# The second layer's first FFN product as whole float32 matmuls instead of three matmuls of split parts

## The chip, the cores and the metric

The kernel runs on one core of one Trainium2 chip. A core has a tensor engine (PE, with PEld for its loads of stationary operands), a vector engine (DVE), a scalar engine (ACT), GpSimd (POOL) and a queue engine (SP) that issues most transfers here. The metric is the device time of one execution in microseconds (us); lower is better. Two executions of the kernel before took 2526.02 and 2526.43 us, median 2526.22 us.

## The reference

The reference is a trunk of two residual layers over 256 tokens of width 2048, all in float32. Each layer has a mixer (layer 0: retention and neighbourhood attention; layer 1: differential attention), a cross-attention into 256 memory tokens and a SwiGLU feed-forward network (FFN). What matters here is the FFN and its place:

```python
def swiglu_ffn(h, w_in, w_out):
    g, u = jnp.split(h @ w_in, 2, axis=-1)
    return (jax.nn.silu(g) * u) @ w_out

for i in range(DEPTH):                 # DEPTH = 2
    ...
    x = x + memory_cross_attention(rms_norm(x, norm_xattn_g[i]), m, ...)
    x = x + swiglu_ffn(rms_norm(x, norm_ffn_g[i]), w_ffn_in[i], w_ffn_out[i])
```

`h` is 256 x 2048, `w_ffn_in[i]` is 2048 x 11264 and `w_ffn_out[i]` is 5632 x 2048. The first FFN product is `h @ w_in`.

## The kernel before

**Split products.** The large products are not made of float32 matmuls. Each float32 operand is split into a high part, which is the value rounded to the type float32r, and a low part, which is the rest, also in float32r. One product of a 128x128 stationary tile and a 128x512 moving tile then takes three matmuls that add into the same accumulator: high by high, high by low, low by high (lines 318, 319, 320). In the FFN product the stationary operand is `hT`, the normed and transposed activations (`hTfh` and `hTfl` in the profile), and the moving operand is the weights (`wh` and `wl`). The whole-float32 form of a matmul occurs in one place only, the retention heads (line 539, `pa_r <- vh, dm`), where both operands are plain float32 tiles of 128x128.

**The weight stream.** All weights go through one stream. `plan` lists the products as phases; a phase is a matrix, its row groups of 512, its column groups of 512 and the order of its units. A unit is two row tiles of 128 against one group of 512 columns, for both halves of the 256 tokens. `prepare()` brings the next unit: for each second unit it allocates one of three `raw` buffers of 1 MB (pool `rawp`) and issues the transfer on SP (line 284); then ACT makes the high part `wh` by a cast (line 291) and DVE makes the low part `wl` by a subtraction (line 293). Both have pools of three buffers. `gemm()` keeps three units prepared (`LOOK = 2`, and the one in use), and makes a unit's matmuls: 2 halves of the tokens x 2 row tiles x 3 parts = 12.

**The order around it.** `Side` holds side work (transposes of the activations, attention heads, norms) and places steps of it between units. A scheduler then sets the order within each engine. The first FFN product of a layer runs in three groups of column blocks, `FFN_GROUPS = ((0, 4), (4, 8), (8, 11))`, each followed by the part of the second FFN product that uses them. It has 22 column groups x 8 units = 176 units per layer, so 176 x 4 = 704 pairs of tiles, each with three matmuls. A column group ends in `epi_in` (silu on ACT, line 782, or a multiplication on DVE), which reads the accumulator.

**The activations.** `feed()` transposes blocks of `x`, and `gained()` writes them with the norm's gain into `hT`: the high part by ACT (line 347), the low part by DVE (line 348). For the FFN of one layer there are 16 such pairs.

Of the kernel before, what the change touches and what calls it, by code (L numbers as in the profile page):

```python
# [10 lines left out]
F32 = mybir.dt.float32  # L11
# [5 lines left out]
P = 128  # L17
D = 2048
T = 256
# [8 lines left out]


class Side:  # L30
    """Steps of generators, placed after units of the weight stream. A step yields the units to wait before
    the next one, or (units, what has to hold)."""

    CAP = 5

# [43 lines left out]
def trunk_kernel(  # L79
# [8 lines left out]
    nc = tc.nc  # L88
# [18 lines left out]
    ps_t = pool("ps_t", 2, space=bass.MemoryType.PSUM)  # L107
    ps_a = pool("ps_a", 2, space=bass.MemoryType.PSUM)

    # ---------------------------------------------------------------- loads  # L110
    x_sb = const.tile([P, 2, D], F32, name="x_sb")
    x_v = x[0].rearrange("(t p) d -> p t d", p=P)
    def load_x(b):
# [12 lines left out]
    nc.gpsimd.iota(tdiff, pattern=[[-P, 2], [1, T]], base=0, channel_multiplier=-1,  # L126
                   allow_small_or_imprecise_dtypes=True)
    tabs = tdiff
    # columns of the grid outside the window of each query's column, in both halves of the partitions
    wmask = const.tile([P, 64], F32, name="wmask")  # L130
    nc.gpsimd.memset(wmask, 0.0)
    for q in range(2):
# [42 lines left out]
            nc.vector.tensor_scalar(hcol[:, c:c + n], hcol[:, c:c + n], f, None, op0=ALU.mult)  # L175

    def decays():
        # log_sigmoid(y) = -(max(-y, 0) + log1p(exp(-|y|))), log1p(e) = 2 atanh(e / (2 + e))
        dec = sm.tile([P, 16], F32, name="dec")
        nc.scalar.dma_start(dec[:, 0:8], dec_f.broadcast_to([P, 8]))  # L180
        nc.scalar.dma_start(dec[:, 8:16], dec_b.broadcast_to([P, 8]))
        e_t = sm.tile([P, 16], F32, name="e_t")
        z_t = sm.tile([P, 16], F32, name="z_t")
        z2 = sm.tile([P, 16], F32, name="z2")
        pl = sm.tile([P, 16], F32, name="pl")
        nc.vector.scalar_tensor_tensor(out=e_t, in0=dec, scalar=-1.0, in1=dec, op0=ALU.mult, op1=ALU.min)
        nc.scalar.activation(e_t, e_t, AF.Exp)
        nc.vector.tensor_scalar(z_t, e_t, 2.0, None, op0=ALU.add)
        nc.vector.reciprocal(z_t, z_t)
        nc.vector.tensor_mul(z_t, z_t, e_t)  # L190
        nc.vector.tensor_mul(z2, z_t, z_t)
        nc.vector.tensor_scalar(pl, z2, 2.0 / 17.0, 2.0 / 15.0, op0=ALU.mult, op1=ALU.add)
        for n in (13, 11, 9, 7, 5, 3, 1):
            nc.vector.tensor_mul(pl, pl, z2)
            nc.vector.tensor_scalar(pl, pl, 2.0 / n, None, op0=ALU.add)
        nc.vector.tensor_mul(pl, pl, z_t)
        nc.vector.tensor_scalar(nlg, dec, -1.0, 0.0, op0=ALU.mult, op1=ALU.max)
        nc.vector.tensor_add(nlg, nlg, pl)
        nc.vector.tensor_scalar(lg, nlg, -1.0, None, op0=ALU.mult)
        return  # L200
        yield
# [14 lines left out]
        return  # L216
        yield

    # ------------------------------------------------------------- helpers
    def pair(which, name):  # L220
        hi = big.tile([P, 16, T], F32R, tag=f"{which}h", name=f"{name}h")
        lo = big.tile([P, 16, T], F32R, tag=f"{which}l", name=f"{name}l")
# [6 lines left out]
    LOOK = 2  # L229

    def woven(nblocks, nu, early, lead=2):
        """The first `lead` blocks do their early units first."""
        head = [(b, u) for b in range(lead) for u in range(early)]
        head += [(b, u) for b in range(lead) for u in range(early, nu)]
        return head + [(b, u) for b in range(lead, nblocks) for u in range(nu)]

    # the weight stream: (matrix, row groups, column groups, order of (column group, unit))
    plan = []

    def phase(w2, rows, cols, order=None):  # L240
        nu = 2 * len(rows)
        plan.append((w2, rows, cols, order or [(b, u) for b in range(len(cols)) for u in range(nu)]))

    four = tuple(b * NB for b in range(4))
# [5 lines left out]
    for layer in range(2):  # L250
        j = layer // 2
        if layer % 2 == 0:
            phase(w_in_ab[j], K4, cols_ab, start)
            phase(w_out_ab[j], (1024, 1536, 0, 512), four, woven(4, 8, 6))
        else:
            phase(w_in_c[j], K4, cols_c, woven(len(cols_c), 8, 6))
            phase(w_out_c[j], K4, four, woven(4, 8, 6))
        phase(w_xkv[layer], K4, (0,))
        phase(w_xq[layer], K4, (0,))
        phase(w_xkv[layer], K4, (NB,))  # L260
        phase(w_xo[layer], (0,), four, woven(4, 2, 1))
        for g0, g1 in FFN_GROUPS:
            n = 2 * (g1 - g0)
            cols = [c + b * NB for b in range(g0, g1) for c in (0, HID)]
            phase(w_ffn_in[layer], K4, cols, woven(n, 8, 6) if g0 == 0 else None)
            phase(w_ffn_out[layer], tuple(b * NB for b in range(g0, g1)), four, woven(4, n, n - 2))
    units = [(i, b, u) for i, ph in enumerate(plan) for b, u in ph[3]]
    ahead = deque()
# [1 line left out]
    at = {"unit": 0, "phase": 0}  # L270

    def prepare():
        """The next unit of weights, two row groups of 128, in its two parts."""
        i, b, u = units[at["unit"]]
        w2, rows, cols, _ = plan[i]
        c, h = u // 2, u % 2
        if (i, b, c) not in raws:
            raw = raws[i, b, c] = rawp.tile([P, 4, NB], F32, name="raw")
            src = w2[rows[c]:rows[c] + 512, cols[b]:cols[b] + NB].rearrange("(k p) n -> p k n", p=P)
            if at["unit"] == 0:  # L280
                nc.sync.dma_start(raw[:, 0:2], src[:, 0:2])
                nc.sync.dma_start(raw[:, 2:4], src[:, 2:4])
            else:
                nc.sync.dma_start(raw, src)
        if at["unit"] in (1, 5, 9):
            load_x(at["unit"] // 4 + 1)
        raw = raws[i, b, c]
        if h:
            del raws[i, b, c]
        wh = hip.tile([P, 2, NB], F32R, name="wh")  # L290
        nc.scalar.copy(wh, raw[:, 2 * h:2 * h + 2])  # L291
        wl = lop.tile([P, 2, NB], F32R, name="wl")
        nc.vector.tensor_sub(wl, raw[:, 2 * h:2 * h + 2], wh)  # L293
        ahead.append((wh, wl))
        at["unit"] += 1

    def gemm(kts, src, epi, gate=None, steps=1):
# [5 lines left out]
        for b, u in order:  # L303
            side.drain((gate or {}).get(u, ()))
            if b not in accs:
                accs[b] = [ps_acc.tile([P, NB], F32, tag=f"acc{t}", name=f"acc{t}") for t in range(2)]
                left[b] = nu
            while len(ahead) <= LOOK and at["unit"] < len(units):
                prepare()
            wh, wl = ahead.popleft()  # L310
            acc = accs[b]
            first, left[b] = left[b] == nu, left[b] - 1
            last = left[b] == 0
            for t in range(2):
                ts = slice(t * P, (t + 1) * P)
                for j in range(2):
                    kt = kts[u // 2] + 2 * (u % 2) + j
                    nc.tensor.matmul(acc[t], lhsT=hi[:, kt, ts], rhs=wh[:, j], start=first and j == 0, stop=False)  # L318
                    nc.tensor.matmul(acc[t], lhsT=hi[:, kt, ts], rhs=wl[:, j], start=False, stop=False)  # L319
                    nc.tensor.matmul(acc[t], lhsT=lo[:, kt, ts], rhs=wh[:, j], start=False, stop=last and j == 1)  # L320
            if last:
                epi(b, acc)
            side.pump(steps)
# [19 lines left out]
        return pt  # L343

    def gained(dst, kt, src, g):
        hi, lo = dst[0][:, kt], dst[1][:, kt]
        nc.scalar.activation(hi, src, AF.Copy, scale=g)
        nc.vector.scalar_tensor_tensor(out=lo, in0=src, scalar=g, in1=hi.bitcast(F32),  # L348
# [15 lines left out]
        yield  # L364

    def feed_x(dst, b, gi, layer, ssr, wait=0):
        """The steps that bring block b of x, transposed and with its gain, into dst."""
        then = (lambda: finish_rstd(ssr)) if b == 3 else None
        t0 = side.add(feed(dst, b, 0, x_block(b), gi, layer, ssr), wait)
        return [t0, side.add(feed(dst, b, 1, x_block(b), gi, layer, ssr, then), wait + 1, finished([t0]))]  # L370
# [3 lines left out]
        nc.vector.tensor_sub(lo, src, hi)  # L374

    def product(out, lhs, rhs, start, stop):
        """out += lhs.T @ rhs, each given in its two parts."""
        (lh, ll), (rh, rl) = lhs, rhs
        nc.tensor.matmul(out, lhsT=lh, rhs=rh, start=start, stop=False)  # L379
        nc.tensor.matmul(out, lhsT=lh, rhs=rl, start=False, stop=False)  # L380
# [3 lines left out]
        return tuple(x[(slice(None),) + index] for x in pair)  # L384

    def gained_pair(dst, src, g):
        """Both parts of src * g."""
        hi, lo = dst
        nc.scalar.activation(hi, src, AF.Copy, scale=g)
        dims = "p a b -> p (a b)"  # L390
# [99 lines left out]
        return att_pair(pt)  # L490

    def attend(g, h, dst, kt, bias=None):
        """One head of softmax attention; g holds qT, kT and, later, v."""
        ps = scores(g["q"], g["k"], h)
        pr = att.tile([P, 2, T], F32, tag="att", name="pr")
        if bias is not None:
# [12 lines left out]
            product(po, part(v, s, slice(h * HD, (h + 1) * HD)), part(pT, s), s == 0, s == 1)  # L509
        split(dst[0][:, kt], dst[1][:, kt], po)  # L510

    # -------------------------------------------------------- even mixer
    def na_bias(j, gi, g, behind=None):
        bias = g["bias"] = m8.tile([P, 4, 2, T], F32, tag="m8", name="bias")
        if behind is not None:  # the table comes in behind what is needed sooner
            nc.gpsimd.tensor_copy(bias[:, 0, :, 0:8], behind.rearrange("p (t c) -> p t c", t=2))
        for t in range(2):
            for q in range(2):
# [83 lines left out]
        side.drain(tails[:1])  # L602
        return {6: tails}

    # --------------------------------------------------------- odd mixer
    def diff_head(g, hh, h, j, oT):
        slope = 2.0 ** (-8.0 * (h + 1) / 8)
        prs = []
# [57 lines left out]
            side.drain(groups[b]["tasks"])  # L666
        return {6: groups[3]["tasks"]}

    # ------------------------------------------------------------ norms
    def new_ss(name):  # L670
        return (sm.tile([P, 2, 4], F32, name=name), sm.tile([P, 2], F32, name=name + "r"),
                sm.tile([P, 2], F32, name=name + "q"))
# [11 lines left out]
        for t, xb in enumerate(x_block(b)):  # L684
            nc.vector.tensor_tensor(xb, acc[t], xb, op=ALU.add)

    # ------------------------------------------------------------ trunk
    which = "AB"
    hT = pair(which[0], "hT")
    ssr = new_ss("ssx")  # L690
# [8 lines left out]
    for layer in range(2):  # L699
# [50 lines left out]
        xo = (xo[:, 0], xo[:, 1])  # L750
        heads = [side.add(attend(g, h, xo, h), cond=prepared(g)) for h in range(4)]
        gemm(KT4, mT, epi_v, steps=2)
        hT = pair(B, "hTf")
        ssr = new_ss("ssx")
        tasks = []

# [82 lines left out]
```

## Time and profile before

| | |
|---|---|
| median of the runs, us | 2526.22 (2526.02 to 2526.43) |
| span of the profiled execution, us | 2523.3 |
| PE busy in the span, us (share) | 2506.5 (99%) |
| PEld busy, us (share) | 2077.9 (82%) |
| DVE busy, us (share) | 1428.8 (57%) |
| ACT busy, us (share) | 1191.3 (47%) |
| mean granted clock of the tensor engine | 1.000 |
| mean rate of the transfers | 185 GB/s |

The profiled execution's time is its span, 2523.3 us, from the first to the last instruction. The median of the runs is 2.9 us longer: what lies around the span. The duration of a matmul in the profile runs from its start to its modelled end. Matmuls overlap, so in a stream the distance from one start to the next (the pitch) is what one costs, and not its duration.

### The profile page before, as it was taken

Reading aid. Unit: us, or ns where it says so; the run is one execution under the profiler, and the core shown is the slowest. Engines: PE = TensorE matmul, PEld = TensorE weight load, DVE = VectorE, ACT = ScalarE, POOL = GpSimd, SP = SyncE. Lnnn points to the kernel's source line nnn. Section 1 sums busy time; section 2 is a strip of 40 time slices with the busy share of each in tenths; the row PEclk is TensorE's granted clock in tenths of the full one; section 3 lists DMA queues with packets and bytes.
Section 4 is the critical chain, followed back from the end, with each engine's and each line's share of the span. In section 5 each row is a group of like instructions: output and inputs, shape, how many; then the busy total and the mean of one; then the engine's idle time right before and its main releaser. Section 6 shows DMA issues by size and latency. Waiting matters only on the chain.

```text
span 2523.3 us, 28920 instructions
## 1 busy us (share of the span) xinstructions
PE 2506.5 (99%) x11603; PEld 2077.9 (82%) x11603; DVE 1428.8 (57%) x1686; ACT 1191.3 (47%) x1553; POOL 50.2 (2%) x56
## 2 busy tenths in 40 slices
PE   8999999999999999999999999999999999999999
PEld 6888888888888888888888888888888888888887
DVE  5775555674555445545557766757654545545454
ACT  5554455564443444344445545655544344443443
POOL 1000000000000000000000000000000000000000
PEclk9999999999999999999999999999999999999999
DMA  7555555545555555555555555554555565555555
GB/s 235 171 174 177 179 191 185 178 155 193 186 186 198 186 197 184 195 189 189 193 183 167 168 167 171 196 184 155 179 185 198 185 199 185 188 195 189 194 185 165
DMA packets 234509, 465.69 MB, mean 185 GB/s; under 512 B 7931, under 2 KB 8582, under 8 KB 234374
## 3 DMA queue, kind: packets, MB, share of 16 engines
q1 hardware_dynamic: 231552, 459.32, 55.3%
q0 software_dynamic: 640, 2.10, 0.4%
q10 hardware_dynamic: 2182, 2.42, 0.3%
q8 instruction: 91, 1.49, 0.3%
q14 instruction: 44, 0.36, 0.0%
HBM read 461.71 MB, written 2.10 MB: 184 GB/s over the span
## 4 chain that ended last, share of the span: by engine, by line
PE 97%; DMA 1%; DVE 1%; ACT 0%; POOL 0%; issue 0%; SPq 0%; ACTq 0%; DVEq 0%; POOLq 0%
PE acc L318 31%; PE acc L320 31%; PE acc L319 31%; PE pt L342 3%; PE pt L489 0%; PE pa_s L381 0%; PE pa_s L380 0%; PE pa_s L379 0%; DMA x_sb<-in_x 0%; DMA bias<-in_na_rpb 0%; PE pa_r L539 0%; DMA mb<-in_mem 0%; DMA lrow<-in_lambda_k 0%; DVE wl L293 0%; PE pa_o L381 0%
## 5 line engine op out<-in xcount | busy, mean ns | idle before, releaser
L293 DVE TENSOR_TENSOR wl<-raw,wh 128x1024 fp32r<-128x1024 f32 x864 | 1056.2, 1224 | 962.8 <-ACT wh L291 962.6
L291 ACT CAST wh<-raw 128x1024 fp32r<-128x1024 f32 x864 | 909.3, 1052 | 1178.0 <-PE acc L320 1158.8
L318 PE MATMUL acc<-wh,hTfh 128*128 128x512 f32 x1408 | 551.5, 392 | 0.0
L320 PE MATMUL acc<-wh,hTfl 128*128 128x512 f32 x1408 | 548.2, 389 | 0.0
L319 PE MATMUL acc<-wl,hTfh 128*128 128x512 f32 x1408 | 547.8, 389 | 0.0
L318 PE MATMUL acc<-wh,hTh 128*128 128x512 f32 x832 | 332.6, 400 | 2.7 <-DVE z L419 1.5
L320 PE MATMUL acc<-wh,hTl 128*128 128x512 f32 x832 | 325.7, 391 | 1.1 <-DVE hTl L348 1.0
L319 PE MATMUL acc<-wl,hTh 128*128 128x512 f32 x832 | 325.0, 391 | 0.0
L320 PEld LDWEIGHTS acc<-wh,hTfl 128*128 128x128 f32 x1408 | 264.3, 188 | 55.4
L319 PEld LDWEIGHTS acc<-wl,hTfh 128*128 128x128 f32 x1408 | 264.5, 188 | 53.7
L318 PEld LDWEIGHTS acc<-wh,hTfh 128*128 128x128 f32 x1408 | 264.4, 188 | 53.6
L318 PE MATMUL acc<-wh,aTh 128*128 128x512 f32 x704 | 275.5, 391 | 0.0
L320 PE MATMUL acc<-wh,aTl 128*128 128x512 f32 x704 | 274.4, 390 | 0.0
L319 PE MATMUL acc<-wl,aTh 128*128 128x512 f32 x704 | 274.1, 389 | 0.0
L320 PEld LDWEIGHTS acc<-wh,hTl 128*128 128x128 f32 x832 | 156.5, 188 | 36.3 <-DVE hTl L348 2.4
L318 PEld LDWEIGHTS acc<-wh,hTh 128*128 128x128 f32 x832 | 156.9, 189 | 33.2 <-issue 2.3
L319 PEld LDWEIGHTS acc<-wl,hTh 128*128 128x128 f32 x832 | 157.2, 189 | 28.6
L320 PEld LDWEIGHTS acc<-wh,aTl 128*128 128x128 f32 x704 | 132.3, 188 | 27.4
L319 PEld LDWEIGHTS acc<-wl,aTh 128*128 128x128 f32 x704 | 132.2, 188 | 26.9
L318 PEld LDWEIGHTS acc<-wh,aTh 128*128 128x128 f32 x704 | 132.2, 188 | 26.9
L318 PE MATMUL acc<-wh,oTh 128*128 128x512 f32 x256 | 101.9, 398 | 0.0
L320 PE MATMUL acc<-wh,oTl 128*128 128x512 f32 x256 | 99.9, 390 | 0.0
(193 smaller groups left out, 1915.7 us busy)
## 6 DMA issues: line engine op xcount, KB each, us to landing
raw<-in_w_ffn_in SPq DMA_DIRECT2D x176, 1024.0 KB, 5.1
raw<-in_w_ffn_out SPq DMA_DIRECT2D x88, 1024.0 KB, 5.1
raw<-in_w_in_ab SPq DMA_DIRECT2D x55, 1024.0 KB, 5.3
raw<-in_w_in_c SPq DMA_DIRECT2D x48, 1024.0 KB, 5.1
raw<-in_w_out_ab SPq DMA_DIRECT2D x16, 1024.0 KB, 5.1
raw<-in_w_xkv SPq DMA_DIRECT2D x16, 1024.0 KB, 5.0
raw<-in_w_out_c SPq DMA_DIRECT2D x16, 1024.0 KB, 5.2
raw<-in_w_xq SPq DMA_DIRECT2D x8, 1024.0 KB, 5.3
```

The source lines that it names most:

```text
L291: nc.scalar.copy(wh, raw[:, 2 * h:2 * h + 2])
L293: nc.vector.tensor_sub(wl, raw[:, 2 * h:2 * h + 2], wh)
L318: nc.tensor.matmul(acc[t], lhsT=hi[:, kt, ts], rhs=wh[:, j], start=first and j == 0, stop=False)
L319: nc.tensor.matmul(acc[t], lhsT=hi[:, kt, ts], rhs=wl[:, j], start=False, stop=False)
L320: nc.tensor.matmul(acc[t], lhsT=lo[:, kt, ts], rhs=wh[:, j], start=False, stop=last and j == 1)
L342: nc.tensor.transpose(pt[:, j, t * P:(t + 1) * P], srcs[t][:, c:c + P], ident)
```

## The change

The phases of the second layer's first FFN product are marked as whole. For these, `prepare()` makes no `wh` and `wl`; it hands the half of the `raw` buffer on as it is. `gemm()` then makes one matmul in float32, with the `raw` buffer as moving operand, for each three of before. The activations `hT` of this product are one float32 tile (`hTw`) without a low part, so `gained()` makes one instruction instead of two. The first layer and all other products keep the split.

```diff
-    def phase(w2, rows, cols, order=None):
+    whole = set()
+
+    def phase(w2, rows, cols, order=None, is_whole=False):
         nu = 2 * len(rows)
+        if is_whole:
+            whole.add(len(plan))
         plan.append((w2, rows, cols, order or [...]))
...
-            phase(w_ffn_in[layer], K4, cols, woven(n, 8, 6) if g0 == 0 else None)
+            phase(w_ffn_in[layer], K4, cols, woven(n, 8, 6) if g0 == 0 else None, is_whole=layer == 1)
...
         if h:
             del raws[i, b, c]
+        if i in whole:
+            ahead.append((raw[:, 2 * h:2 * h + 2], None))
+            at["unit"] += 1
+            return
         wh = hip.tile([P, 2, NB], F32R, name="wh")
...
                     kt = kts[u // 2] + 2 * (u % 2) + j
+                    if wl is None:
+                        nc.tensor.matmul(acc[t], lhsT=hi[:, kt, ts], rhs=wh[:, j], start=first and j == 0,
+                                         stop=last and j == 1)
+                        continue
                     nc.tensor.matmul(acc[t], lhsT=hi[:, kt, ts], rhs=wh[:, j], start=first and j == 0, stop=False)
...
     def gained(dst, kt, src, g):
+        if dst[1] is None:
+            nc.scalar.activation(dst[0][:, kt], src, AF.Copy, scale=g)
+            return
...
-        hT = pair(B, "hTf")
+        if layer == 0:
+            hT = pair(B, "hTf")
+        else:
+            hT = big.tile([P, 16, T], F32, tag=f"{B}h", name="hTw"), None
```

The rest of the edit takes out comments, which shifts line numbers: the weight transfer is line 288 after, the whole matmul line 327, the split ones 330 to 332, a transpose of `feed()` 354.

The first place is the start of the second layer's first FFN product on PE. `pt` are transposes of `x` for the last blocks of `hT`, `acc_...` the accumulators of the first column group for one half of the tokens each. Before, the rows read:

```order
L342 MATMUL pt<-ident,x_sb 128x128 x3
L318 MATMUL acc_13732<-wh,hTfh 128x512 [waits Activation_49]
L319 MATMUL acc_13732<-wl,hTfh 128x512
L320 MATMUL acc_13732<-wh,hTfl 128x512
L318 MATMUL acc_13732<-wh,hTfh 128x512
```

After the change the rows at the same place, with a whole unit between two lots of transposes, read:

```order
L354 MATMUL pt<-ident,x_sb 128x128 x3
L327 MATMUL acc_13711<-raw,hTw 128x512 [waits DMAHW3_49]
L327 MATMUL acc_13711<-raw,hTw 128x512
L327 MATMUL acc_13712<-raw,hTw 128x512 x2
L354 MATMUL pt<-ident,x_sb 128x128 [waits DVE_49,Activation_49]
L354 MATMUL pt<-ident,x_sb 128x128 [waits DVE_49]
L354 MATMUL pt<-ident,x_sb 128x128 x2
```

A unit is now four matmuls in the program where it was twelve, and the first of them waits for the transfer itself (`DMAHW3`) where the first of before waited for ACT's cast.

The second place is SP's queue where the first of the three groups ends and the second product's weights (`in_w_ffn_out`) begin. The names in brackets are what a transfer waits for: an earlier transfer's semaphore, and the engine that frees the buffer. Before:

```order
L284 DMA raw<-in_w_ffn_in 128x4x512 [waits DMAHW6_49,DVE_49]
L284 DMA raw<-in_w_ffn_in 128x4x512 [waits DMAHW7_49,DVE_49]
L284 DMA raw<-in_w_ffn_out 128x4x512 [waits DMAHW0_49,DVE_49]
L284 DMA raw<-in_w_ffn_out 128x4x512 [waits DMAHW1_49,DVE_49]
L284 DMA raw<-in_w_ffn_out 128x4x512 [waits DMAHW2_49,DVE_49]
L284 DMA raw<-in_w_ffn_out 128x4x512 [waits DMAHW3_49,DVE_49]
```

After:

```order
L288 DMA raw<-in_w_ffn_in 128x4x512 [waits DMAHW6_49,PE_49]
L288 DMA raw<-in_w_ffn_in 128x4x512 [waits DMAHW7_49,PE_49]
L288 DMA raw<-in_w_ffn_out 128x4x512 [waits DMAHW0_49,PE_49]
L288 DMA raw<-in_w_ffn_out 128x4x512 [waits DMAHW1_49,PE_49]
L288 DMA raw<-in_w_ffn_out 128x4x512 [waits DMAHW3_49,DVE_49]
L288 DMA raw<-in_w_ffn_out 128x4x512 [waits DMAHW2_49,PE_49]
L288 DMA raw<-in_w_ffn_out 128x4x512 [waits DMAHW4_49,DVE_49]
```

Inside the product, and for the first transfers behind it, a buffer is now freed by PE, when the last matmul that reads it is done, where DVE freed it when `wl` was made. The third and fourth transfers of the second product have changed places in the queue.

## The prediction

> **What bounds the kernel now.** I read the page first: its head, the clock row and the chain of work that ended last.
>
> ```profile
> span 2523.3 us, 28920 instructions
> PE 2506.5 (99%) x11603; PEld 2077.9 (82%) x11603; DVE 1428.8 (57%) x1686; ACT 1191.3 (47%) x1553; POOL 50.2 (2%) x56
> PEclk9999999999999999999999999999999999999999
> PE 97%; DMA 1%; DVE 1%; ACT 0%; POOL 0%; issue 0%; SPq 0%; ACTq 0%; DVEq 0%; POOLq 0%
> ```
>
> PE is busy 99% of the span, at its full granted clock, and 97% of the chain is PE. Work taken from another engine gives nothing here; PE's own time decides. The stretch that holds the changed product (from the end of the second layer's attention to the end) shows the same in the windows view. Its columns are the window, its length, then the busy time of each engine, clock, share and rate of the transfers.
>
> ```profile
> 1763.20:2523.30 760.10, 756.21 (x3397) 625.74 (x3397) 386.42 (x371) 322.17 (x351) 0.69 (x1) 1.00 0.57 187
> 2519.44 0.69 DVE x_sb L685
> ```
>
> Of 760.1 us PE is idle 3.9, and the chain's last row (start, duration) says that 2523.3 - 2519.4 = 3.9 us of the stretch lie behind PE's last work. So no stall is left there that the change could remove. The groups of the costliest instructions name the work:
>
> ```profile
> L293 DVE TENSOR_TENSOR wl<-raw,wh 128x1024 fp32r<-128x1024 f32 x864 | 1056.2, 1224 | 962.8 <-ACT wh L291 962.6
> L291 ACT CAST wh<-raw 128x1024 fp32r<-128x1024 f32 x864 | 909.3, 1052 | 1178.0 <-PE acc L320 1158.8
> L318 PE MATMUL acc<-wh,hTfh 128*128 128x512 f32 x1408 | 551.5, 392 | 0.0
> L320 PE MATMUL acc<-wh,hTfl 128*128 128x512 f32 x1408 | 548.2, 389 | 0.0
> L319 PE MATMUL acc<-wl,hTfh 128*128 128x512 f32 x1408 | 547.8, 389 | 0.0
> ```
>
> 1408 is both layers; the second has 704 triples. What a triple costs is its pitch, from the timeline (start, duration) inside the product:
>
> ```profile
> 1900.03 0.39 PE L318 MATMUL acc<-wh,hTfh 128*128 128x512 f32 x1
> 1900.25 0.39 PE L319 MATMUL acc<-wl,hTfh 128*128 128x512 f32 x1
> 1900.48 0.39 PE L320 MATMUL acc<-wh,hTfl 128*128 128x512 f32 x1
> 1900.71 0.39 PE L318 MATMUL acc<-wh,hTfh 128*128 128x512 f32 x1
> ...
> 1911.59 0.39 PE L318 MATMUL acc<-wh,hTfh 128*128 128x512 f32 x1
> ```
>
> 17 triples lie between the first row and the last: 11.56 / 17 = 0.680 us per triple, 0.2267 us per split matmul.
>
> **The change, part by part.** (1) It removes 704 triples, 704 x 0.680 = 478.7 us, all of it on the path.
>
> (2) It adds 704 whole float32 matmuls of 128x512. No row shows one of that size; the same form at 128 columns is line 539, and beside it stand the one-pass matmuls of 256 columns and the float32 transposes:
>
> ```profile
> L539 PE MATMUL pa_r<-vh,dm 128*128 128x128 f32 x64 | 8.9, 277 | 0.0
> L379 PE MATMUL pa_s<-kTh,qTh 128*128 128x256 f32 x64 | 18.0, 281 | 0.0
> L342 PE MATMUL pt<-ident,sg 128*128 128x128 f32 x192 | 28.7, 272 | 0.0
> L169 PE MATMUL pt_g<-ident,gr 96*128 96x96 f32 x1 | 0.2, 246 | 0.0
> 1353.47 0.28 PE L379 MATMUL pa_s<-kTh,qTh 128*128 128x256 f32 x1
> 1353.59 0.28 PE L380 MATMUL pa_s<-kTl,qTh 128*128 128x256 f32 x1
> 1353.71 0.28 PE L381 MATMUL pa_s<-kTh,qTl 128*128 128x256 f32 x1
> ```
>
> First, the number of instructions. Line 539 is called for 8 heads x 2 x 2 = 32 products and the trace has 64: a whole float32 matmul is two instructions on the chip, each with its load. Second, what one of them takes. The split matmuls have a pitch of 0.120 us at 256 columns and 0.2267 at 512, so a column of one pass costs 0.1067 / 256 = 0.417 ns and 13 ns are fixed. At 128 columns a one-pass matmul would then last 281 - 128 x 0.417 = 228 ns, but line 539 shows 277, the duration of 256 columns. The transposes agree: from 96 to 128 columns the duration grows by 26 ns, 0.81 ns per column, twice 0.417. I read this as two passes over the columns in each float32 instruction, four per product. Third, the fixed part, from the back-to-back row of line 539 (PE, and the loads that go with it):
>
> ```profile
> 242.56 0.94 PE L539 MATMUL pa_r<-vh,dm 128*128 128x128 f32 x6
> 242.55 0.74 PEld L539 LDWEIGHTS pa_r<-vh,dm 128*128 128x128 f32 x6 [0.29 <-ACT vh L461]
> L539 PEld LDWEIGHTS pa_r<-vh,dm 128*128 128x128 f32 x64 | 8.5, 191 | 1.2 <-ACT vh L461 0.6
> ```
>
> Six loads span 0.74 us and one lasts 0.191, so the pitch is 0.55 / 5 = 0.110 us for 128 columns. Two passes of 128 columns are 256 x 0.417 = 107 ns, which leaves 3 ns, not 13. For 512 columns the bounds are 1024 x 0.417 = 427 ns with nothing fixed, and 4 x 110 = 440 with the fixed part in each quarter. I take 427 + 3 = 430 ns, since the fixed part of line 539 is per instruction. A product then costs 0.860 us against 0.680, and the change 704 x 0.180 = +126.7 us (0.854: +122.5; 0.880: +140.8).
>
> The Trainium skill, in "FP8 and Floating Point Precision", section "TensorE Precision Notes", says that a true float32 matmul makes four passes, high and low of each side, the product of the two low parts included; three split matmuls leave that one out. By this rule the change cannot win, and line 539's doubled instructions with doubled durations agree. In "TensorE: Matmul & The Clock Gate", section "Back-to-back issue gap", it gives N / 2.4 + 2.5 ns for a warm matmul, 215.8 for 512 columns, where the trace has 226.7 for the split form, so the measurement decides there; as an estimate from that page, an instruction of two passes is 429.2 ns and the change 704 x (0.8584 - 0.680) = +125.6 us.
>
> (3) Loads: two per product instead of three. They were hidden (PEld overlaps PE), and at a pitch of 0.110 us one fits under 0.430 us of matmul. Zero; a load out in the open is a rival below.
>
> (4) ACT loses 176 casts of 1.052 us, DVE 176 subtractions of 1.224 us and 16 of the 32 low parts of activations:
>
> ```profile
> L348 DVE SCALAR_TENSOR_TENSOR hTfl<-pt,gcol,hTfh x32: 472/476/484, 547.2 to 1801.3; 128x256 fp32r<-128x256 f32 x32
> ```
>
> That is 185 us of ACT and 215 + 8 us of DVE. All of it lay beside PE (ACT 47%, DVE 57% busy). Zero.
>
> (5) The buffers. A `raw` buffer is now free only when PE has finished with it. Two units share a buffer and there are three, so a transfer for units 2r and 2r+1 starts at the end of unit 2r-5 and has four units of cover. A unit is four products, 3.44 us: 13.8 us of cover. The need:
>
> ```profile
> raw<-in_w_ffn_in SPq DMA_DIRECT2D x176, 1024.0 KB, 5.1
> L284 SPq DMA_DIRECT2D raw<-in_w_ffn_in x176: 367/368/368, 538.9 to 2431.1; - x176
> DMA to landing us min/median/max: 4.9/5.1/9.2
> ```
>
> 0.4 us to issue and 5.1 to land, 9.2 at worst: hidden. SP has nothing but weights in this stretch, so what queues behind a waiting transfer is the next weights, and PE waits for them last. The tightest place is where the second product starts: its third transfer (behind the fourth in the queue) needs the buffer of the last whole units, starts when they end, and its units are the fifth and sixth of that product. The cover is four split units of 4 x 0.680 = 2.72 us, 10.9 us; the need is 5.5, then 1.05 for the cast and 1.22 for the subtraction, 7.8 us. Zero, and if that cover is short, about the 2.3 us of preparation at each of three such places, 7 us at most.
>
> The sum: 2523.3 + 126.7 = 2650.0 us of span, and with the 2.9 us that the runs' median has above the span 2652.9. With the bounds and the 7 us of part 5, 2648.7 to 2674.0; I begin at 2646 for the hundredths by which the pitches are read.
>
> **The rivals.**
>
> *Faster: one pass per instruction.* If each of the two instructions streams its 512 columns once at today's pitch, a product costs 2 x 0.2267 = 0.453 us: 704 x (0.453 - 0.680) = -160 us, 2366 us. For it: the pitch of 0.110 us in line 539 could be that of the loads alone, and ends of matmuls are modelled. Against: the duration of 277 ns, and the transposes' slope. It decides where a product takes under 0.680 us, that is, an instruction under 0.340. 6%.
>
> *No change: three passes.* If the product of the two low parts is left out by the hardware, a product is 3 x 0.2135 + 0.006 = 0.647 us: 704 x (-0.033) = -23 us, 2503 us. Against: both instructions of line 539 last alike. 2%.
>
> *Slower: 13 ns in each pass.* If each of the four passes costs the 0.2267 us of today's matmul, a product is 0.907 us: +160 us, 2686 us. Against: the 0.110 us of line 539 leaves no room for that. 8%.
>
> *Slower: a load out in the open.* If the second load of a product waits for the first instruction's end, each of 1408 instructions pays 0.110 us: +155 us on top, 2808 us. Nothing of the kind shows in line 539, whose PE row has no idle time. 3%.
>
> *Slower: the weights come late.* If a buffer came free so late that one unit of cover was left, each of 88 transfers would cost 5.5 - 3.44 = 2.1 us: +181 us on top, 2834 us. It decides where landing takes over 13.4 us, above all landings seen. 2%.
>
> *The change does not do what it says:* the 704 matmuls run as one split matmul each, 704 x (0.2267 - 0.680) = -319 us, 2207 us. Line 539, from plain float32 tiles, is doubled, so hardly. 1%.
>
> **How the numbers follow.** The forecast has 78%, and its time is 2653 us. To leave out no more than 2 in 10 the range takes in the nearest rival, 2686: 2646 to 2688 holds 86%. About 2% (50 us) is what a measurement of this kernel tells from no change. Faster: 6 + 1 = 7%. Within 2%: 3%, with a point for what lies between the cases. Slower: the rest, 90%.
>
> **What the profile after would show.** 1408 instructions of line 327 in place of 2112, and 11603 - 704 = 10899 on PE; their pitch 0.430 us; PE still 99% busy at full clock, some 127 us longer; ACT near 1191 - 185 = 1006 us and DVE near 1429 - 215 - 8 = 1206 us, with no gain from it. A pitch near 0.227 or 0.453 gives the rival of that size; idle time of PE ahead of line 327 put down to `raw` gives the late weights; a granted clock under 1.00 in the stretch would be a cause that I have not priced. I am wrong if 512 columns of float32 take a different number of passes than the 128 of line 539.

## The result and the profile after

The changed kernel takes 2652.35 us (2651.98 to 2652.71) against 2526.22 us before: a ratio of 1.0498, 95% interval 1.0479 to 1.0518. It is slower by 126.1 us, where +126.7 us was forecast.

The head of the page after, its clock row, the chain by engine and by line, and the costliest groups of the changed product read:

```profile
span 2650.2 us, 26921 instructions
PE 2631.7 (99%) x10899; PEld 1949.3 (74%) x10899; DVE 1210.9 (46%) x1494; ACT 1008.6 (38%) x1377; POOL 50.2 (2%) x56
PEclk9999999999999999999999999999999999999999
PE 98%; DMA 1%; DVE 1%; ACT 0%; POOL 0%; issue 0%; ACTq 0%; SPq 0%; DVEq 0%; POOLq 0%
...
L327 PE MATMUL acc<-raw,hTw 128*128 128x512 f32 x1408 | 607.7, 592 | 0.0
L327 PEld LDWEIGHTS acc<-raw,hTw 128*128 128x128 f32 x1408 | 266.0, 190 | 326.9 <-issue 326.7
```

PE has 704 instructions less and 125.2 us more busy time (2631.7 against 2506.5). It still fills 99% of the span at its full clock, while DVE and ACT lost 217.9 and 182.7 us. The last column of the matmul row is PE's idle time ahead of it: 0.0 us in 1408 instructions. That rules out long waits, for `raw` say, but not short ones: a matmul lasts 592 ns to its modelled end and the next one starts after 429, so a wait of up to 163 ns would not show as idle time. It is the pitch that rules out the short ones. The loads' own idle time, 326.7 us put down to "issue", is the loads waiting their turn behind matmuls that have become longer.

The pitch is read from the chain in order of time (start, length, work):

```profile
1799.39 51.50 PE acc L327 x120
1850.89 0.44 PE pt L354 x4
1851.33 3.43 PE acc L327 x8
```

51.50 / 120 = 0.4292 us per instruction, 0.8584 us per product of two instructions, against 0.680 us for the triple: 704 x 0.1784 = +125.6 us. Two passes over 512 columns at the prediction's 0.417 ns are 427 ns, so some 2 ns of the 429 are left for all else: no load lies in the open. The span grew by 126.9 us, but about 2 us of that arose ahead of the changed product. In the view by tile, the last transfer of the weights just ahead of it is issued at 1763.6 us before (first row) and at 1765.5 us after:

```profile
L284 SPq DMA_DIRECT2D raw<-in_w_xo x8: 367/368/368, 512.0 to 1763.6; - x8
L288 SPq DMA_DIRECT2D raw<-in_w_xo x8: 367/368/368, 514.1 to 1765.5; - x8
```

The shift is there from the first layer on (512.0 against 514.1 for the same matrix), where the change does nothing. So the changed product and what follows it took about 125 us more, close to the 125.6 us of the pitch.

The prediction's stretch, from the same start time to the end, in the windows view (window, length, then the busy time of each engine; by the shift it begins 1.9 us earlier in the program than before):

```profile
1763.20:2650.20 887.00, 882.95 (x2706) 498.42 (x2705) 169.93 (x180) 141.05 (x178) 0.70 (x1) 1.00 0.48 160
```

887.0 us against 760.1, with PE idle for 4.05 us against 3.9. The stretch was full of matmuls before and is full of them now.

### The profile page after: what moved, and what is told of

It reads as the page before. It is cut to its first block, busy times and chain, and to the rows that moved or that the text cites. A ratio compares the mean times of both kernels' runs of the same rounds, so it can differ in the third digit from the quotient of the medians.

```text
span 2650.2 us, 26921 instructions
## 1 busy us (share of the span) xinstructions
PE 2631.7 (99%) x10899; PEld 1949.3 (74%) x10899; DVE 1210.9 (46%) x1494; ACT 1008.6 (38%) x1377; POOL 50.2 (2%) x56
## 4 chain that ended last, share of the span: by engine, by line
PE 98%; DMA 1%; DVE 1%; ACT 0%; POOL 0%; issue 0%; ACTq 0%; SPq 0%; DVEq 0%; POOLq 0%
PE acc L330 23%; PE acc L332 23%; PE acc L331 23%; PE acc L327 23%; PE pt L354 2%; DMA x_sb<-in_x 0%; PE pt L504 0%; PE pa_s L396 0%; PE pa_s L395 0%; PE pa_s L394 0%; DMA lrow<-in_lambda_k 0%; PE pa_r L554 0%; DVE wl L301 0%; PE pa_o L396 0%; PE pa_o L395 0%; PE pa_d L396 0%
## 5 line engine op out<-in xcount | busy, mean ns | idle before, releaser
L301 DVE TENSOR_TENSOR wl<-raw,wh 128x1024 fp32r<-128x1024 f32 x688 | 840.5, 1224 | 834.0 <-ACT wh L299 833.6
L299 ACT CAST wh<-raw 128x1024 fp32r<-128x1024 f32 x688 | 723.5, 1052 | 974.6 <-PE acc L332 888.3
L327 PE MATMUL acc<-raw,hTw 128*128 128x512 f32 x1408 | 607.7, 592 | 0.0
L327 PEld LDWEIGHTS acc<-raw,hTw 128*128 128x128 f32 x1408 | 266.0, 190 | 326.9 <-issue 326.7
L330 PE MATMUL acc<-wh,hTfh 128*128 128x512 f32 x704 | 275.8, 392 | 0.0
L332 PE MATMUL acc<-wh,hTfl 128*128 128x512 f32 x704 | 274.1, 389 | 0.0
L331 PE MATMUL acc<-wl,hTfh 128*128 128x512 f32 x704 | 273.9, 389 | 0.0
L803 DVE SCALAR_TENSOR_TENSOR sg<-acc,ssxr,sg 128x512 f32<-128x512 f32 x44 | 31.9, 747 | 400.6 <-PE acc L327 400.6
L332 PEld LDWEIGHTS acc<-wh,hTfl 128*128 128x128 f32 x704 | 132.1, 188 | 27.7
L331 PEld LDWEIGHTS acc<-wl,hTfh 128*128 128x128 f32 x704 | 132.2, 188 | 26.9
```

Source lines behind the costliest of these rows:

```text
L803: nc.vector.scalar_tensor_tensor(out=sgs[blk][t], in0=acc[t], scalar=r1[:, t:t + 1], in1=sgs[blk][t], op0=ALU.mult, op1=ALU.mult)
```

## The experiments

My theory: a whole float32 product is four passes over its columns in two instructions, PE's time alone decides, and all else that the change does is hidden. The rivals, run by run, are that buffers and waits make the difference, that it belongs to the place in the program, or that the work taken from ACT and DVE did count.

**A fourth matmul in the split form.** The arithmetic of the whole form, low by low included, in split matmuls, without the changed buffers. The cut is against the kernel before; `four_parts` holds in the phases that the change marks as whole:

```diff
                     nc.tensor.matmul(acc[t], lhsT=lo[:, kt, ts], rhs=wh[:, j], start=False, ...)
+                    if four_parts:
+                        nc.tensor.matmul(acc[t], lhsT=lo[:, kt, ts], rhs=wl[:, j], start=False, ...)
```

> The split kernel with a fourth matmul, low by low, in each product of the second layer's first FFN product; nothing else of the change is in it. My theory (a whole float32 product is four passes over 512 columns, and the tensor engine's time alone decides): 704 more matmuls at the split pitch of 0.2267 us, 2526.2 + 159.6 = 2685.8 us, so 33 us above the whole form, whose pitch after is 0.4292 us per instruction of two passes. Rival (the 126 us of the change come from what it does to buffers and waits, and a pass is not what is paid): a fourth pass without those would stay clearly below 2652 us.

Measured: 2685.68 us (2684.72 to 2686.38), ratio 1.0632 (1.0616 to 1.0648). The timeline (start, duration) has the four parts of a product at the old pitch: 1900.04 to 1901.85 is eight matmuls, 1.81 us, or 0.905 us for each four, where 4 x 0.2267 is 0.907:

```profile
1900.04 0.39 PE L325 MATMUL acc<-wh,hTfl 128*128 128x512 f32 x1
1900.27 0.39 PE L328 MATMUL acc<-wl,hTfl 128*128 128x512 f32 x1
1900.49 0.39 PE L322 MATMUL acc<-wh,hTfh 128*128 128x512 f32 x1
1900.72 0.39 PE L323 MATMUL acc<-wl,hTfh 128*128 128x512 f32 x1
...
1901.85 0.39 PE L325 MATMUL acc<-wh,hTfl 128*128 128x512 f32 x1
```

One split matmul more per product costs its pitch, 159.6 us in all, with the old buffers and waits; passes are what is paid. And the whole form is 33 us cheaper than four split matmuls.

**Both layers whole.**

```diff
-... is_whole=layer == 1)
+... is_whole=True)
```

In the same edit `hTw` takes the place of the pair `hTf` in the first layer too.

> The first layer's first FFN product is made whole as well. My theory (a price per product, wherever it stands): another 704 x (0.8584 - 0.680) = 125.6 us, 2652.4 + 125.6 = 2778 us. Rival (part of the 126 us belongs to the place, the end of the program with its waits for weights): the first layer would cost a different amount, away from 2778 by over 5 us.

Measured: 2776.84 us (2775.68 to 2777.93), ratio 1.0993 (1.0977 to 1.101). Beside the changed kernel's 2652.35 us, the first layer's product costs +124.5 us; the second's cost +126.1. In the chain of this kernel the same row stands in both layers:

```profile
569.68 51.50 PE acc L327 x120
1302.10 48.07 PE acc L327 x112
```

48.07 / 112 is 0.4292 us again. The price goes by product, not by place.

**The split work kept, unread.** The whole matmuls stay; ACT and DVE make `wh` and `wl` of these weights as before.

```diff
             ahead.append((raw[:, 2 * h:2 * h + 2], None))
             at["unit"] += 1
+            wh = hip.tile([P, 2, NB], F32R, name="wh")
+            nc.scalar.copy(wh, raw[:, 2 * h:2 * h + 2])
+            wl = lop.tile([P, 2, NB], F32R, name="wl")
+            nc.vector.tensor_sub(wl, raw[:, 2 * h:2 * h + 2], wh)
             return
```

> The changed kernel, whole matmuls included, but the cast on ACT and the subtraction on DVE are made for these weights all the same and nobody reads them: 176 x 1.05 us of ACT and 176 x 1.22 us of DVE come back. My theory (that work lay beside the tensor engine, and taking it away gave nothing): 2652 us, within 3. Rival (taking it away did give something, and the matmuls cost more than I think): the time rises above 2652 by that gain, 5 us or more.

Measured: 2652.31 us (2650.55 to 2653.05), ratio 1.0501 (1.0484 to 1.0519). Its engine row beside that of the changed kernel above:

```profile
PE 2631.3 (99%) x10899; PEld 1948.9 (74%) x10899; DVE 1417.2 (54%) x1670; ACT 1181.7 (45%) x1553; POOL 50.3 (2%) x56
```

206 us of DVE and 173 us of ACT are back, and the medians differ by 0.04 us where the runs of this kernel alone scatter by 2.5 us. What the change takes from these two engines is worth nothing that shows.

**Two parts.** The split form without high by low; the low part of these weights is left out of the computation, so this is less work and not the same work done faster. The cut is against the kernel before; `prepare()` makes no `wl` in these phases.

```diff
-                    nc.tensor.matmul(acc[t], lhsT=hi[:, kt, ts], rhs=wl[:, j], start=False, stop=False)
+                    if wl is not None:
+                        nc.tensor.matmul(acc[t], lhsT=hi[:, kt, ts], rhs=wl[:, j], start=False, stop=False)
```

> The split kernel without the matmul high by low in the second layer's first FFN product, and without the low part of its weights: that part of the computation is left out. My theory (each pass removed is worth its pitch): 704 x 0.2267 = 159.6 us less, 2366.6 us. Rival (with units of 1.81 us the weights come late, since a pair of units takes 1 MB in 3.63 us, 289 GB/s, and no slice of the profile before moved more than 235 GB/s): 88 transfers at 235 GB/s take 4.46 us each, 0.83 us more than the matmuls, and the gain shrinks by 73 us to about 2440 us.

Measured: 2367.96 us (2367.15 to 2368.52), ratio 0.9374 (0.936 to 0.9388). The rival that weights come late falls: the stretch, in the windows view, has PE busy for 599.17 of 603.20 us, and the transfers (last column) run at 235 GB/s in the mean, where the kernel before had 187.

```profile
1763.20:2366.40 603.20, 599.17 (x2712) 495.69 (x2711) 177.17 (x197) 322.46 (x354) 0.70 (x1) 1.00 0.71 235
```

The rival took the 235 GB/s of the busiest slice before as a limit, but that was only what that kernel asked for: slices of this run reach 280 GB/s.

**One part.** High by high alone: the low parts of these weights and of their activations are left out of the computation. In the edit a product without `wl` makes the matmul of `hi` and `wh` and goes on to the next.

> One matmul per product, high by high, in the second layer's first FFN product; the low parts of its weights and activations are left out of the computation. The tensor engine alone would need 176 units of 0.907 us, 160 us instead of 479, 2207 us in all. My theory: it is no longer the bound. ACT's casts of 1.05 us per unit make it 185 us, 2232 us; the transfers, 88 of 1 MB, make it more: 393 us at the 235 GB/s of the busiest slice before, 2440 us, or 281 us at the 328 GB/s that 187 GB/s at a 57% share would reach at 100%, 2328 us. I expect between these two. Rival (the transfers keep up): 2207 to 2232 us.

Measured, in one execution without an interval: 2303.04 us. Here the mechanism changed as expected and the size did not fit: I had put the time between 2328 and 2440 us. Row by row: the rate of the transfers in 40 slices of the span; the stretch; two windows that lie wholly in the changed product (the last three columns are the granted clock, the DMA engines' busy share and GB/s); and a pair of casts from the timeline that waits for a transfer (in brackets, idle time before and what ended it):

```profile
GB/s 239 170 177 170 179 183 188 183 167 162 188 197 183 194 189 193 191 183 200 184 194 190 183 165 176 165 153 183 202 173 167 302 342 186 286 343 211 264 321 164
1763.20:2301.20 538.00, 476.57 (x2012) 364.17 (x2010) 177.12 (x199) 312.20 (x355) 0.70 (x1) 0.97 0.76 264
1800.00:1850.00 50.00, 37.99 (x147) 24.70 (x146) 5.75 (x9) 37.61 (x43) 0.00 (x0) 0.97 0.97 346
2192.00:2230.00 38.00, 30.71 (x112) 21.46 (x112) 3.58 (x6) 28.51 (x32) 0.00 (x0) 0.91 0.99 353
2178.14 1.99 ACT L295 CAST wh<-raw 128x1024 fp32r<-128x1024 f32 x2 [0.91 <-DMA raw<-in_w_ffn_in]
```

Now PE is idle for 61 us of 538. In the changed product the transfers run at some 350 GB/s with their engines 97 to 99% busy, so the weights are the bound there. My limit of 328 GB/s, the rate that a share of 57% would make at 100%, was too low. The Trainium skill, in "DMA: Bandwidth & Descriptors", section "Where 436 GB/s comes from", puts the limit of one core's share of the memory at about 358 GB/s; the 346 and 353 here lie just under it, but no run shows that this limit is what binds. The run is also 96 us above the 2207 us that PE alone would need, more than PE's idle time: the granted clock fell to 0.97 and 0.91 in the two windows, a cause that I had not priced, and waits that end under a modelled matmul do not show. How the rest divides between the two stays open.

**Half the columns.** Each whole matmul of 512 columns is made as two of 256:

```diff
-                        nc.tensor.matmul(acc[t], lhsT=hi[:, kt, ts], rhs=wh[:, j], ...)
+                        for c in range(0, NB, NB // 2):
+                            nc.tensor.matmul(acc[t][:, c:c + NB // 2], lhsT=hi[:, kt, ts],
+                                             rhs=wh[:, j, c:c + NB // 2], ...)
```

> The changed kernel with each whole matmul of 512 columns made as two of 256. My theory (427 ns of columns and a fixed 2.5 ns per instruction): a product becomes four instructions of 213.3 + 2.5 ns, 0.8633 us instead of 0.8584, 704 x 0.0049 = +3.5 us, about 2656 us. Rival (the fixed part is that of the split form, 13 ns): +10.8 ns in each of four instructions and more, 0.906 us, +33 us, about 2686 us. Rival (the load is not hidden): twice as many loads of 0.110 us in the open, +155 us.

Measured: 2654.51 us (2654.12 to 2655.83), ratio 1.0508 (1.0494 to 1.0522), which the runs alone do not tell from the changed kernel's 1.0498. The chain tells it:

```profile
2167.62 51.80 PE acc L328 x240
```

51.80 / 240 = 0.2158 us. With 0.4292 us at 512 columns this is 0.8336 ns per column, twice the 0.417 of a one-pass column, and 2.4 ns fixed: the two passes and a small fixed part hold at these sizes, and twice the loads, 190 ns each, stay hidden.

**Two buffers for the weights.** `pool("rawp", 3)` becomes `pool("rawp", 2)`, for all phases.

> The changed kernel with two buffers for the weights' transfers instead of three, in all phases. By my count of the cover a transfer of the whole product then starts two units of 3.43 us ahead of its use, 6.9 us, against 5.5 us of need; in the split phases a buffer is free once the low part is made, some five units of 2.72 us ahead of the use, 13.6 us, against 5.5 + 2.3 of need at the third unit of preparation, 10.1 us with the preparation that frees it. So no wait in the steady stream: 2652 us within 5, the first units of a phase aside. Rival (the cover is smaller than I count, and weights come late when a buffer is held by the tensor engine): the tensor engine waits ahead of whole matmuls, 1 us or more at each of 88 transfers, 2740 us or more.

Measured: 2658.71 us (2658.09 to 2660.38), ratio 1.0525 (1.0508 to 1.0542), some 6 us over the changed kernel and a little more than my 5. A stretch of the whole product in the windows view, a run of it in the chain, and the waits of PE over the whole span that speak of weights (total us, times, longest):

```profile
1794.60:1962.50 167.90, 167.90 (x412) 75.60 (x411) 7.66 (x14) 10.77 (x19) 0.70 (x1) 1.00 0.43 144
1802.62 51.50 PE acc L327 x120
PE acc L331 <- DVE wl L301: 1.5, 7, 0.3
```

PE has no idle time in that stretch, and the whole matmuls keep their pitch (51.50 / 120), even with one buffer less; the few short waits are at split units, for a low part. One of them belongs to the transfer that I called the tightest, the one that takes the buffer of the last whole units. The chain has it, then its cast and its subtraction, and the timeline has the matmul that waited:

```profile
2018.15 5.09 DMA raw<-in_w_ffn_out
2023.27 1.06 ACT wh L299
2024.35 1.24 DVE wl L301
2025.63 0.50 PE L331 MATMUL acc<-wl,aTh 128*128 128x512 f32 x1 [0.22 <-DVE wl L301]
```

The need is 7.4 us here, where I had put 7.8. With two buffers its cover is two split units, 5.4 us, and PE waits; with three it is four, 10.9 us, and in the changed kernel the view of waits shows none of PE from 1763 us on. Inside the whole product the cover of 6.9 us with two buffers suffices, so the 13.8 us with three do, and the rival of late weights falls. About half of the 6 us arise ahead of the changed product, whose first load is at 1794.6 us here and at 1791.4 us with three buffers.

**The parts in bfloat16.** Three matmuls as before, but high and low parts of weights and activations of this product in bfloat16, so with fewer bits than the float32r parts carry:

```diff
-        wh = hip.tile([P, 2, NB], F32R, name="wh")
+        dt = BF16 if i in whole else F32R
+        wh = hip.tile([P, 2, NB], dt, name="wh")
...
-        hT = pair(B, "hTf")
+        hT = pair(B, "hTf") if layer == 0 else tuple(
+            big.tile([P, 16, T], BF16, tag=f"{B}{x}", name=f"hTb{x}") for x in "hl")
```

> The split kernel with the high and low parts of the second layer's first FFN product, of weights and of activations, in bfloat16 instead of float32r; three matmuls per product as before, so each part carries fewer bits. The split float32r matmul has 13 ns beside its columns (0.2267 us at 512, 0.120 at 256), the whole float32 instruction 2.5 (0.4292 at 512, 0.2158 at 256). My theory (the 13 ns belong to the type float32r): a pitch near 0.216 us, 704 x 3 x 0.0108 = 23 us less than before, 2503 us. Rival (they belong to streams in which each pass has a load of its own, whatever the type): the pitch stays at 0.227 us and the time at 2526 us. ACT and DVE write half the bytes for this product; by the run that kept their unread work that is worth nothing.

Measured: 2503.54 us (2502.22 to 2504.29), ratio 0.991 (0.9893 to 0.9926). In the timeline 18 triples, 54 matmuls, lie between these two rows, 11.65 / 54 = 0.2157 us each:

```profile
1900.09 0.38 PE L325 MATMUL acc<-wl,hTbh 128*128 128x512 bf16 x1
...
1911.74 0.38 PE L325 MATMUL acc<-wl,hTbh 128*128 128x512 bf16 x1
```

The same number of passes and of loads, 22.5 us less, under 1% but clear of the scatter: most of the fixed 13 ns of the split form goes away with the type float32r.

## Why the prediction was right

**The bound.** PE alone decides: keeping the ACT and DVE work changed nothing, and adding a pass cost 159.6 us, the price of its pitch. The steps that put parts (3) to (5), loads, casts and buffers, at zero hold; what shows it is the pitch with the half columns, the run with unread split work and the run with two buffers.

**The term that carried it.** The step from the 128 columns of line 539 to 512 was the one without a row of its own. It gave 0.430 us and the trace has 0.4292, so the term was 1.1 us too large. The error is in the fixed part: 3 ns from the pitch of line 539, where the pair of 256 and 512 columns gives 2.4. The estimate from "TensorE: Matmul & The Clock Gate" of the Trainium skill, section "Back-to-back issue gap", which gives the gap of an isolated matmul, was +125.6 us, and that is what the pitch after gives. The trace agrees also with four passes, as "FP8 and Floating Point Precision" of the Trainium skill, section "TensorE Precision Notes", says of a true float32 matmul. The pitch alone cannot tell two passes of an instruction from one pass at half the rate; the price is the same.

**What was luck.** The pitch of 0.110 us was read in hundredths over five steps, which leaves some 2 ns either way, or 3 us in the sum, so an error of 1.1 us is better than that reading could promise. The median's close fit to 2653 owes something to luck too, since the span moves by some 2 us at places that the change does not touch.

**Two readings that were weaker than they sound.** The prediction says that line 539 has doubled durations. Its instructions last 277 ns against the 228 ns that one pass would last; it is the 128 columns' part of the duration that doubles, not the whole. And the slope of the transposes rests on one instruction of 96 columns. The same view has one of 32 columns that lasts 283 ns, longer than the 246 of the 96, so a slope across these single instructions shows little:

```profile
L146 PE MATMUL pt_g<-ident,gr 32*128 32x32 f32 x1 | 0.3, 283 | 2.7 <-DMA gr<-in_norm_mix_g 2.7
```

What carried the two passes was the duration of line 539, equal to that of a matmul of 256 columns, and its pitch.

**The rivals.** One pass per instruction needed a pitch near 0.227 us, 13 ns in each pass one near 0.453, and three passes a product of 0.647 us; the trace has 0.4292 and 0.8584. The load out in the open is refuted by that pitch and by the half columns, which doubled the loads for 2 to 4 us; the prediction's sign, no idle time in the row of line 539, could not show it, since a matmul there lasts 277 ns and the pitch is 110. That the change does not do what it says is refuted by 1408 instructions of line 327. The upper bound of 440 ns, a fixed part in each quarter, was wider than needed: the fixed part is per instruction.

**The smaller forecasts.** 10899 PE instructions came out to the one; ACT at 1008.6 us against 1006 and DVE at 1210.9 against 1206 are close.

**What the experiments leave.** The two forms that are faster than both kernels, 2368 us with two parts and 2504 us with bfloat16 parts, carry less of the operands into the product. A form that carries as much in less time was not found.

## What to carry to other kernels

Where PE is full, count passes over columns, not instructions or engines relieved: the whole float32 form pays for four passes (0.8584 us here), the split one for three (0.680 us), and ACT and DVE work in PE's shadow is no saving. Where durations overlap, a row without idle time does not show that nothing waits; the pitch does. A form that stands nowhere at the size in question can be priced from its smallest specimen, if its duration and its pitch are read apart: the duration told the passes, the pitch the fixed part. Before holding a buffer longer, count its cover in units of the work that now frees it; here 13.8 us against 5.5 us made it free.

## What the runs showed of the hardware that was not expected

The float32r matmul has about 13 ns beside its columns (0.120 us at 256, 0.2267 at 512), the whole float32 instruction 2.4 ns (0.2158 and 0.4292) and the bfloat16 one about as little (0.2157 us at 512). Three split matmuls pay this 13 ns three times; it is why four passes in the whole form cost 0.8584 us and not 0.907. What causes it is open: no run took it apart further than by the type. The length of the loads is not it alone: bfloat16 loads last 98 ns and float32r loads 188, but in the half columns a load of 190 ns goes with every 0.2158 us, with 2.4 ns over. And the weights' transfers, which in no slice went above 235 GB/s in the kernel before, reached 343 GB/s in a slice when the matmuls asked for it.
